# An adaLN modulation product in plain fp32 on four 32-column groups of the TensorE array, in place of two fp32r parts on the whole array

## The chip, the cores and the metric

The kernel runs on one core of a Trainium2 chip. The metric is the device time of one execution in microseconds; the lower the better. The engines are TensorE (PE; its weight loads are shown as PEld), VectorE (DVE), ScalarE (ACT), GpSimd (POOL) and SyncE (SP), whose queue issues the loads and stores.

## The reference, cut to what matters

One step of a decoder layer for 1024 prompt tokens and 64 sample tokens, model width 2048, all in float32. The modulation comes from a small batch of 9 vectors c (one for the prompt, eight for the samples):

```python
mod = jax.nn.silu(c) @ w_ada + b_ada              # (9, 2048) @ (2048, 6144)
shift, scale, gate = jnp.split(mod[:, None, :], 3, axis=-1)
xn = rmsnorm(x, norm_g) * (1.0 + scale) + shift
z = xn @ w_in                                     # (tokens, 2048) @ (2048, 5120)
...
out = jnp.concatenate([ya, yb, yc], axis=-1) @ w_out
return x + gate * out, new_hist_a, h_last, new_hist_b, vn
```

What lies between z and out are three token mixers (a linear recurrence, a causal convolution, a chunked spatial gate). w_ada is 50 MB, a quarter of all that the kernel loads.

## The kernel before, in words

Activations lie with channels on the 128 partitions and tokens along the free dimension. The tokens are done in two parts, first 512 prompt tokens (T0), then 512 prompt and 64 sample tokens (T1). Each large product is made of fp32r matmuls: an fp32 operand is split into a high part (a cast to fp32r on ScalarE, L98) and the rest (a subtraction on VectorE, L99), and three matmuls add up high x high, high x low and low x high (`mm3`, L132 to L134). The moving operand is the activations, 512 columns for T0.

The modulation product (w_ada) is done the other way round: the stationary operand is c after its SiLU, the moving one is w_ada. The weights are laid out in 24 pieces n of 256 output columns; each piece has 4 blocks b of 512 KB, and each block holds 4 tiles of 128 rows (k = 4b + j) side by side. n = 0 to 7 give shift, 8 to 15 scale, 16 to 23 gate.

- `cs` (L92, filled at L138 to L143) holds for each k 18 columns, the high part of 9 vectors and the low part of the same; `ada_mm` takes 128 columns from there as the stationary operand, of which the first 18 count.
- `ada_block` (L683) loads a block to a ring of 6 buffers ("ar"), splits it in two halves to high and low on ScalarE and VectorE, and calls `ada_mm`: 4 x 2 matmuls with 256 columns, which all add to one PSUM tile, high and low rows apart.
- `ada_fin` (L164) copies rows 0 to 18 of that tile to SBUF, and turns them by two small fp32 matmuls against `sel`, which adds high and low rows (`ps_adat`, L170); VectorE adds the bias and writes `adam`, the modulation by channel.
- `gate_block` (L156) does the same for n = 16 to 23, later: after each half of a `single` product of part T0 from the 19th on, one block, loaded and split by `load_w` (L101).

The first stage (the loop `for i in range(9)` near the end) goes through i = 0 to 8: the blocks of n = i and n = 8 + i, and, from i = 1 on, the normalised activations 2(i-1) and 2(i-1)+1 (`norm_pair`) and their first projection step (`k_step`: 18 matmuls with 512 columns to `ps_g`). The statistics of the norm need all 16 tiles of x (`load_x0`: squares on ScalarE, 14 additions on VectorE into two accumulators, then L711 adds these two), a reduction on TensorE (`ps_var`, L211) and a row broadcast (`ps_bc`, L202). 18 small VectorE steps of a softplus series (`sw`) are independent of all that.

The order on each engine is set by a scheduler that takes priorities (`tc.high_priority`) and the readiness of data as it estimates it; each engine then works strictly by its list.

Of the kernel before, what the change touches and what calls it, by code (L numbers as in the profile page):

```python
# [8 lines left out]
F32 = mybir.dt.float32  # L9
F32R = mybir.dt.float32r  # L10
AF = mybir.ActivationFunctionType
ALU = mybir.AluOpType
PSUM = bass.MemoryType.PSUM

P = 128
KT = 16
# [4 lines left out]
TM = T1  # L21
# [22 lines left out]
def decoder_layer(ctx: ExitStack, tc: tile.TileContext, a):  # L44
    nc = tc.nc

    cpool = ctx.enter_context(tc.tile_pool(name="cpool", bufs=1))
    xp = ctx.enter_context(tc.tile_pool(name="xp", bufs=17))
# [10 lines left out]
    HP = 4000  # L59
# [15 lines left out]
    ident = cpool.tile([P, P], F32, name="ident")  # L75
    make_identity(nc, ident)
    sel = cpool.tile([P, 9], F32, name="sel")
    nc.vector.tensor_tensor(sel[0:18, :], ident[0:18, 0:9], ident[0:18, 9:18], op=ALU.add)
    one_d = cpool.tile([P, 1], F32, name="one_d")
    nc.gpsimd.memset(one_d, 1.0 / 2048.0)  # L80
    one_c = cpool.tile([P, P], F32, name="one_c")
# [7 lines left out]
    car_h = cpool.tile([P, 8], F32, name="car_h")  # L89
    car_glu = cpool.tile([P, 4, 30], F32, name="car_glu")  # L90
    hs_out = cpool.tile([P, 8, 8], F32, name="hs_out")
    cs = cpool.tile([P, KT * 18 + 110], F32R, name="cs")  # L92
    nc.gpsimd.memset(car_xa, 0.0)
    nc.gpsimd.memset(car_h, 0.0)
    nc.gpsimd.memset(car_glu, 0.0)
# [1 line left out]
    def split(raw, hi, lo):  # L97
        nc.scalar.copy(hi, raw)  # L98
        nc.vector.tensor_tensor(lo, raw, hi.bitcast(F32), op=ALU.subtract)  # L99
# [35 lines left out]

    with tc.high_priority(10 * HP):
        sg = ap.tile([P, KT, 9], F32, tag="sg", name="sg", bufs=1)
        nc.scalar.activation(sg, cT, AF.Sigmoid)  # L138
        nc.vector.tensor_tensor(sg, sg, cT, op=ALU.mult)
        nc.gpsimd.memset(cs[:, KT * 18:].bitcast(F32), 0.0)  # L140
        cs3 = cs[:, :KT * 18].rearrange("p (k n) -> p k n", n=18)
        nc.scalar.copy(cs3[:, :, 0:9], sg)
        nc.vector.tensor_tensor(cs3[:, :, 9:18], sg, cs3[:, :, 0:9].bitcast(F32), op=ALU.subtract)  # L143

    def ada_mm(ps, b, hl):
        for j in range(4):
            k = 4 * b + j
            st = cs[:, k * 18:k * 18 + P]
            hi, lo = hl[j // 2]
            c = slice((j % 2) * 256, (j % 2) * 256 + 256)  # L150
            nc.tensor.matmul(ps, st, hi[:, c], start=(k == 0), stop=False)  # L151
            nc.tensor.matmul(ps, st, lo[:, c], start=False, stop=(k == 15))  # L152

    gate_ps = {}

    def gate_block(f):  # L156
        n, b = 16 + f // 4, f % 4
        if b == 0:
            gate_ps[n] = pmm.tile([P, 2, 512], F32, tag="mm", name="ps_ada")[:, 0, :256]
        ada_mm(gate_ps[n], b, load_w(a["w_ada"][n, b], 1024, 2))  # L160
        if b == 3:
            ada_fin(n, gate_ps[n])

    def ada_fin(n, ps):  # L164
        rows = stp.tile([P, 256], F32, tag="rows", name="rows", bufs=1)
        with tc.high_priority(HP):
            nc.scalar.copy(rows[0:18, :], ps[0:18, :])
        pt = mi("ps_adat")
        for j in range(2):
            nc.tensor.matmul(pt[:, j * 9:(j + 1) * 9], rows[0:18, j * P:(j + 1) * P],  # L170
                             sel[0:18, :], start=True, stop=True)
        with tc.high_priority(HP):
            dst = adam[:, n * 2:n * 2 + 2, :]
            o = VEC["b_ada"][0] + n * 2
# [506 lines left out]
    ada_ps = {}  # L681

    def ada_block(n, b):  # L683
        if b == 0:
            ada_ps[n] = mi("ps_ada")[:, :256]
        with tc.high_priority(HP):
            raw = ap.tile([P, 1024], F32, tag="ar", name="w_raw")
            nc.sync.dma_start(raw, a["w_ada"][n, b])
            hl = []
            for j in range(2):  # L690
                hi = xp.tile([P, TM], F32R, tag="xh", name="ada_hi")
                lo = xp.tile([P, TM], F32R, tag="xl", name="ada_lo")
                split(raw[:, j * 512:(j + 1) * 512], hi[:, :512], lo[:, :512])
                hl.append((hi, lo))
        ada_mm(ada_ps[n], b, hl)

    R0 = ap.tile([P, T0], F32, tag="R0", name="R0", bufs=1)
    o = VEC["h0"][0]
# [189 lines left out]
```

## Time and profile before

| what | value |
|---|---|
| median of 3 runs | 1559.56 us (1557.91 to 1559.74) |
| the profiled execution, span from its first to its last instruction | 1557.5 us |
| instructions | 24534 |
| TensorE busy | 1519.7 us, 9388 matmuls |
| TensorE weight loads | 1388.0 us |
| VectorE busy | 1038.4 us |
| ScalarE busy | 702.6 us |
| loaded and stored by DMA | 206.03 MB, mean 132 GB/s |

The profiled execution has no time of its own beside its span; the span lies 2.1 us under the median of the timed runs. Matmuls are pipelined and the end of each record is modelled: a matmul's length in a row is longer than its distance to the next. The distance between starts is what one costs. Each fp32 matmul of the code stands as two matmuls and two weight loads in the trace, an fp32r matmul as one.

### The profile page before, as it was taken

The numbers are of one execution on the slowest core, as the hardware profiler recorded it, in microseconds if no ns is written. First come the engines' busy times: TensorE is split into PE (matmuls) and PEld (weight loads), VectorE is DVE, ScalarE is ACT, GpSimd is POOL, SyncE is SP. The second block draws the span as 40 slices with busy tenths as digits, with TensorE's granted clock in tenths as the row PEclk, the third lists the DMA queues.
The fourth block names the chain that finished last, engine by engine and source line by source line (L and its number), as shares of the span: only waits on it lengthen the run. The fifth ranks groups of instructions, "written<-read, shape, count | busy, mean of one in ns | idle before, by whom it ended". The sixth has DMA issues, their size and how long they took to land.

```text
span 1557.5 us, 24534 instructions
## 1 busy us (share of the span) xinstructions
PE 1519.7 (98%) x9388; PEld 1388.0 (89%) x9388; DVE 1038.4 (67%) x1965; ACT 702.6 (45%) x1211; POOL 52.9 (3%) x120
## 2 busy tenths in 40 slices
PE   5999999999999999999999999999999999999996
PEld 4888788888887888888899999999999999999996
DVE  7888797397878756265595898358866753534345
ACT  6776442244666755244352432226254652422220
POOL 0000000001100100000000010001000000000000
PEclk7999999999999999999999999999999999999998
DMA  8888323323544453366466222222222222234323
GB/s 331 291 289 296 106 81 99 104 85 99 166 156 132 157 163 123 99 202 182 125 200 206 80 76 93 82 82 75 96 89 81 69 72 66 76 113 133 109 85 122
DMA packets 77334, 206.03 MB, mean 132 GB/s; under 512 B 9633, under 2 KB 25633, under 8 KB 77217
## 3 DMA queue, kind: packets, MB, share of 16 engines
q1 hardware_dynamic: 76064, 203.30, 39.5%
q8 instruction: 73, 1.20, 0.3%
q10 hardware_dynamic: 1152, 1.18, 0.2%
q14 instruction: 45, 0.36, 0.1%
HBM read 194.70 MB, written 9.74 MB: 131 GB/s over the span
## 4 chain that ended last, share of the span: by engine, by line
PE 64%; DVE 2%; ACT 1%; issue 0%; DVEq 0%; ACTq 0%
PE ps_s L132 16%; PE ps_s L134 16%; PE ps_s L133 16%; PE ps_g L132 5%; PE ps_g L133 5%; PE ps_g L134 4%; PE ps_bc L202 0%; DVE y L640 0%; PE ps_ada L151 0%; PE ps_ada L152 0%; PE ps_gate L132 0%; PE ps_var L211 0%; PE ps_gate L133 0%; PE ps_gate L134 0%; ACT L441 0%
## 5 line engine op out<-in xcount | busy, mean ns | idle before, releaser
L99 DVE TENSOR_TENSOR w_lo<-w_raw,w_hi 128x512 fp32r<-128x512 f32 (+1 forms) x544 | 351.6, 657 | 385.6 <-PE ps_s L134 239.3
L98 ACT CAST w_hi<-w_raw 128x512 fp32r<-128x512 f32 (+1 forms) x544 | 317.7, 594 | 633.4 <-PE ps_s L133 430.5
L132 PE MATMUL ps_s<-xn_hi,w_hi 128*128 128x288 f32 (+1 forms) x1632 | 535.8, 328 | 2.3 <-ACT pad_a L422 1.2
L133 PE MATMUL ps_s<-xn_lo,w_hi 128*128 128x288 f32 (+1 forms) x1632 | 534.3, 327 | 0.0
L134 PE MATMUL ps_s<-xn_hi,w_lo 128*128 128x288 f32 (+1 forms) x1632 | 533.4, 327 | 0.0
L132 PEld LDWEIGHTS ps_s<-xn_hi,w_hi 128*128 128x128 f32 x1632 | 306.2, 188 | 23.6 <-ACT pad_a L422 1.5
L134 PEld LDWEIGHTS ps_s<-xn_hi,w_lo 128*128 128x128 f32 x1632 | 307.1, 188 | 21.2
L133 PEld LDWEIGHTS ps_s<-xn_lo,w_hi 128*128 128x128 f32 x1632 | 306.5, 188 | 20.8 <-issue 0.5
L359 DVE SCALAR_TENSOR_TENSOR mx<-pad_b,vec,mx 128x512 f32<-128x512 f32 x240 | 177.5, 745 | 2.2
L132 PE MATMUL ps_s<-m_hi,w_hi 128*128 128x288 f32 (+1 forms) x480 | 157.2, 327 | 0.0
L133 PE MATMUL ps_s<-m_lo,w_hi 128*128 128x288 f32 (+1 forms) x480 | 156.7, 326 | 0.0
L134 PE MATMUL ps_s<-m_hi,w_lo 128*128 128x288 f32 (+1 forms) x480 | 156.5, 326 | 0.0
L132 PE MATMUL ps_g<-xn_hi,w_hi 128*128 128x288 f32 (+1 forms) x288 | 94.1, 332 | 2.5 <-ACT xn_hi L227 2.1
L134 PEld LDWEIGHTS ps_s<-m_hi,w_lo 128*128 128x128 f32 x480 | 90.3, 188 | 6.3
L133 PEld LDWEIGHTS ps_s<-m_lo,w_hi 128*128 128x128 f32 x480 | 90.1, 188 | 6.2
L132 PEld LDWEIGHTS ps_s<-m_hi,w_hi 128*128 128x128 f32 x480 | 90.1, 188 | 6.2
L133 PE MATMUL ps_g<-xn_lo,w_hi 128*128 128x288 f32 (+1 forms) x288 | 95.1, 331 | 0.0
L134 PE MATMUL ps_g<-xn_hi,w_lo 128*128 128x288 f32 (+1 forms) x288 | 94.4, 328 | 0.0
L132 PE MATMUL ps_g<-m_hi,w_hi 128*128 128x288 f32 (+1 forms) x288 | 94.1, 328 | 0.1
L133 PE MATMUL ps_g<-m_lo,w_hi 128*128 128x288 f32 (+1 forms) x288 | 94.0, 327 | 0.0
L134 PE MATMUL ps_g<-m_hi,w_lo 128*128 128x288 f32 (+1 forms) x288 | 93.7, 326 | 0.0
L99 DVE TENSOR_TENSOR ada_lo<-w_raw,ada_hi 128x512 fp32r<-128x512 f32 x128 | 80.4, 685 | 6.6 <-ACT ada_hi L98 6.5
(208 smaller groups left out, 1869.6 us busy)
## 6 DMA issues: line engine op xcount, KB each, us to landing
w_raw<-wi_s SPq DMA_DIRECT2D x136, 512.0 KB, 3.5
w_raw<-w_ada SPq DMA_DIRECT2D x96, 512.0 KB, 4.7
w_raw<-wo_s SPq DMA_DIRECT2D x40, 512.0 KB, 3.5
w_raw<-wi_g SPq DMA_DIRECT2D x16, 384.0 KB, 6.1
w_raw<-wo_g SPq DMA_DIRECT2D x16, 384.0 KB, 3.0
w_raw<-wi_g SPq DMA_DIRECT2D x32, 192.0 KB, 2.6
w_raw<-wo_g SPq DMA_DIRECT2D x32, 192.0 KB, 2.3
x_s<-x SPq DMA_DIRECT2D x16, 288.0 KB, 3.3
```

Source lines behind the costliest of these rows:

```text
L98: nc.scalar.copy(hi, raw)
L99: nc.vector.tensor_tensor(lo, raw, hi.bitcast(F32), op=ALU.subtract)
L132: nc.tensor.matmul(out, wh, xh, start=start, stop=False)
L133: nc.tensor.matmul(out, wh, xl, start=False, stop=False)
L134: nc.tensor.matmul(out, wl, xh, start=False, stop=stop)
L359: nc.vector.scalar_tensor_tensor(out[:, :T0], pad[:, j:j + T0], w[:, j:j + 1], out[:, :T0], op0=ALU.mult, op1=ALU.add)
```

## The change

The stationary operand is now a zero-padded fp32 tile `cz` with 32 columns for each k. `ada_mm` makes one plain fp32 matmul of 256 columns per k tile instead of two fp32r ones; the matmul of tile j writes PSUM partitions 32j to 32j + 31, that is, it uses the j-th group of 32 columns of the array. The four groups are added by the small product with `sel`, which now has 128 rows with four ones per column. The weights are no longer split: the casts, subtractions and the high and low tiles of w_ada are gone. In the gate stage a block is loaded in two pieces of 256 KB to a ring of four buffers ("xr") instead of one piece of 512 KB to the ring that the projection weights use.

```diff
-    nc.vector.tensor_tensor(sel[0:18, :], ident[0:18, 0:9], ident[0:18, 9:18], op=ALU.add)
+    nc.vector.tensor_tensor(sel, ident[:, 0:9], ident[:, 32:41], op=ALU.add)
+    nc.vector.tensor_tensor(sel, sel, ident[:, 64:73], op=ALU.add)
+    nc.vector.tensor_tensor(sel, sel, ident[:, 96:105], op=ALU.add)
...
-    cs = cpool.tile([P, KT * 18 + 110], F32R, name="cs")
+    cz = cpool.tile([P, KT, 32], F32, name="cz")
...
+        nc.gpsimd.memset(cz, 0.0)
         nc.scalar.activation(sg, cT, AF.Sigmoid)
         nc.vector.tensor_tensor(sg, sg, cT, op=ALU.mult)
-        nc.gpsimd.memset(cs[:, KT * 18:].bitcast(F32), 0.0)
-        cs3 = cs[:, :KT * 18].rearrange("p (k n) -> p k n", n=18)
-        nc.scalar.copy(cs3[:, :, 0:9], sg)
-        nc.vector.tensor_tensor(cs3[:, :, 9:18], sg, cs3[:, :, 0:9].bitcast(F32), op=ALU.subtract)
-
-    def ada_mm(ps, b, hl):
+        nc.vector.tensor_copy(cz[:, :, 0:9], sg)
+
+    def ada_mm(ps, b, raw):
         for j in range(4):
-            k = 4 * b + j
-            st = cs[:, k * 18:k * 18 + P]
-            hi, lo = hl[j // 2]
-            c = slice((j % 2) * 256, (j % 2) * 256 + 256)
-            nc.tensor.matmul(ps, st, hi[:, c], start=(k == 0), stop=False)
-            nc.tensor.matmul(ps, st, lo[:, c], start=False, stop=(k == 15))
+            nc.tensor.matmul(ps[32 * j:32 * j + 32, :], cz[:, 4 * b + j, :],
+                             raw[j // 2][:, j % 2 * 256:(j % 2 + 1) * 256],
+                             start=(b == 0), stop=(b == 3))
...
-        ada_mm(gate_ps[n], b, load_w(a["w_ada"][n, b], 1024, 2))
+        raw = []
+        with tc.high_priority(HP):
+            for q in range(2):
+                r = sp_.tile([P, TM], F32, tag="xr", name="g_raw")
+                nc.sync.dma_start(r[:, :512], a["w_ada"][n, b][:, q * 512:(q + 1) * 512])
+                raw.append(r)
+        ada_mm(gate_ps[n], b, raw)
...
-            nc.scalar.copy(rows[0:18, :], ps[0:18, :])
+            nc.scalar.copy(rows, ps)
...
-            nc.tensor.matmul(pt[:, j * 9:(j + 1) * 9], rows[0:18, j * P:(j + 1) * P],
-                             sel[0:18, :], start=True, stop=True)
+            nc.tensor.matmul(pt[:, j * 9:(j + 1) * 9], rows[:, j * P:(j + 1) * P],
+                             sel, start=True, stop=True)
...
             nc.sync.dma_start(raw, a["w_ada"][n, b])
-            hl = []
-            for j in range(2):
-                hi = xp.tile([P, TM], F32R, tag="xh", name="ada_hi")
-                lo = xp.tile([P, TM], F32R, tag="xl", name="ada_lo")
-                split(raw[:, j * 512:(j + 1) * 512], hi[:, :512], lo[:, :512])
-                hl.append((hi, lo))
-        ada_mm(ada_ps[n], b, hl)
+        ada_mm(ada_ps[n], b, [raw[:, :512], raw[:, 512:]])
```

The change also moves instructions, since the scheduler no longer sees the splits. On TensorE in the first stage, around the first two projection steps, the matmuls of one n stood between those of the projection before (L151 and L152 are the high and low part of the modulation product, L132 to L134 the projection):

```order
L132 MATMUL ps_g<-xn_hi,w_hi 128x512 x3
L133 MATMUL ps_g<-xn_lo,w_hi 128x512 x2
L134 MATMUL ps_g<-xn_hi,w_lo 128x512
L132 MATMUL ps_g<-xn_hi,w_hi 128x512
L151 MATMUL ps_ada<-ada_hi,cs 128x256
L133 MATMUL ps_g<-xn_lo,w_hi 128x512
L134 MATMUL ps_g<-xn_hi,w_lo 128x512 x2
```

Now the 16 matmuls of one n stand in one piece, here n = 8 + 1 behind the first projection step (L147 is the modulation product, L173 the small product that turns it, L134 to L136 the projection):

```order
L136 MATMUL ps_g<-xn_hi,w_lo 128x512
L147 MATMUL ps_ada<-w_raw,cz 32x256 x16
L173 MATMUL ps_adat<-sel,rows 128x9 x2
L134 MATMUL ps_g<-xn_hi,w_hi 128x512
L135 MATMUL ps_g<-xn_lo,w_hi 128x512
```

The count per n falls from 32 to 16, and full-width and 32-column matmuls alternate by n, no longer one by one.

On TensorE in the gate stage the four matmuls of a block stand between full-width matmuls of a `single` product, as the eight did before:

```order
L135 MATMUL ps_s<-xn_lo,w_hi 128x512
L136 MATMUL ps_s<-xn_hi,w_lo 128x512
L147 MATMUL ps_ada<-g_raw,cz 32x256 x4
L134 MATMUL ps_s<-xn_hi,w_hi 128x512
L135 MATMUL ps_s<-xn_lo,w_hi 128x512
```

There are 32 such blocks, each alone.

On VectorE at the start, the steps of the softplus series (`sw`) stood between the additions of the squares (`acc`) and the subtractions (L99):

```order
L667 TENSOR_TENSOR acc_115<-acc_115,x_sq 128x512
L99 TENSOR_TENSOR ada_lo<-w_raw,ada_hi 128x512
L667 TENSOR_TENSOR acc_114<-acc_114,x_sq 128x512
L667 TENSOR_TENSOR acc_115<-acc_115,x_sq 128x512
L667 TENSOR_TENSOR acc_114<-acc_114,x_sq 128x512
L748 TENSOR_SCALAR sw_2026<-sw_2026 128x8
```

Now all of the series that follows the first `adam` stands ahead of the first addition of the squares:

```order
L178 TENSOR_TENSOR adam<-ps_adat,vec 128x18
L744 TENSOR_TENSOR sw_1259<-sw_1259,sw_1258 128x8
...
L746 TENSOR_TENSOR sw_1259<-sw_1259,sw_1257 128x8
L748 SCALAR_TENSOR_TENSOR sp_100<-sw_1259,sw_1256 128x8
L749 TENSOR_SCALAR sp_100<-sp_100 128x8
L750 TENSOR_SCALAR nsp_101<-sp_100 128x8
L670 TENSOR_TENSOR acc_115<-acc_115,x_sq 128x512
L670 TENSOR_TENSOR acc_116<-acc_116,x_sq 128x512
```

The additions moved behind 18 small steps, and the subtractions between them are gone.

## Rows read from the trace of the kernel before

**Rows 1.** The page, busy time of each engine (share of the span).

```profile
PE 1519.7 (98%) x9388; PEld 1388.0 (89%) x9388; DVE 1038.4 (67%) x1965; ACT 702.6 (45%) x1211; POOL 52.9 (3%) x120
```

**Rows 2.** Stages: length, busy time by engine, granted clock, DMA share, GB/s.

```profile
core 0: us, PE busy (x) PEld busy (x) DVE busy (x) ACT busy (x) POOL busy (x), PEclk, DMA share, GB/s
0.00:40.00 40.00, 22.08 (x112) 20.18 (x113) 29.10 (x78) 28.24 (x52) 1.24 (x12) 0.74 0.89 332
40.00:155.00 115.00, 114.97 (x715) 99.81 (x714) 99.68 (x181) 81.54 (x162) 0.17 (x1) 1.00 0.81 291
386.00:606.00 220.00, 218.71 (x1090) 182.96 (x1089) 164.82 (x269) 144.21 (x238) 15.24 (x25) 1.00 0.46 150
```

**Rows 3.** Timeline of TensorE (start, length), first stage: one n and what follows.

```profile
63.07 0.39 PE L151 MATMUL ps_ada<-ada_hi,cs 128*128 128x256 f32 x1
...
66.95 0.39 PE L132 MATMUL ps_g<-xn_hi,w_hi 128*128 128x512 f32 x1
```

**Rows 4.** Timeline of TensorE, gate stage: one block and what follows.

```profile
387.12 0.28 PE L151 MATMUL ps_ada<-w_hi,cs 128*128 128x256 f32 x1
...
388.07 0.39 PE L132 MATMUL ps_s<-xn_hi,w_hi 128*128 128x512 f32 x1
```

**Rows 5.** Groups by line, 0 to 160 us: busy, mean ns | idle before.

```profile
L99 DVE TENSOR_TENSOR ada_lo<-w_raw,ada_hi 128x512 fp32r<-128x512 f32 x128 | 80.4, 685 | 6.6 <-ACT ada_hi L98 6.5
L98 ACT CAST ada_hi<-w_raw 128x512 fp32r<-128x512 f32 x128 | 70.4, 615 | 9.9 <-PE ps_ada L151 6.8 <-DMA w_raw<-w_ada 3.0
```

**Rows 6.** Timeline of TensorE around the mean of a layernorm, an fp32 matmul.

```profile
176.07 1.10 PE L293 MATMUL ps_mean<-ln_s,one_c 128*128 128x512 f32 x2
176.60 0.79 PE L132 MATMUL ps_s<-xn_hi,w_hi 128*128 128x512 f32 x1
177.24 0.39 PE L133 MATMUL ps_s<-xn_lo,w_hi 128*128 128x512 f32 x1
```

**Rows 7.** Timeline of the weight loads at the same place.

```profile
176.58 0.19 PEld L132 LDWEIGHTS ps_s<-xn_hi,w_hi 128*128 128x128 f32 x1 [0.24 <-issue]
177.01 0.19 PEld L133 LDWEIGHTS ps_s<-xn_lo,w_hi 128*128 128x128 f32 x1 [0.24 <-issue]
177.24 0.19 PEld L134 LDWEIGHTS ps_s<-xn_hi,w_lo 128*128 128x128 f32 x1
```

**Rows 8.** Timeline of TensorE, gate stage: the 18-row matmuls between full ones.

```profile
409.39 0.39 PE L132 MATMUL ps_s<-xn_hi,w_hi 128*128 128x512 f32 x1
409.71 0.61 PE L170 MATMUL ps_adat<-sel,rows 18*128 18x9 f32 x4
410.25 0.50 PE L133 MATMUL ps_s<-xn_lo,w_hi 128*128 128x512 f32 x1
410.58 0.40 PE L134 MATMUL ps_s<-xn_hi,w_lo 128*128 128x512 f32 x1
```

**Rows 9.** Groups by form, weight loads of 96 and of 128 columns.

```profile
L211 PEld LDWEIGHTS ps_var<-one_c,ln_s 128*96 128x96 f32 x24 | 2.2, 165 | 0.0
...
L211 PEld LDWEIGHTS ps_var<-one_c,ln_s 128*128 128x128 f32 x16 | 1.9, 191 | 0.6 <-issue 0.3 <-PE ps_s L133 0.3
```

**Rows 10.** Timeline of TensorE, start: the reduction of the squares (idle before it).

```profile
17.63 0.41 PE L152 MATMUL ps_ada<-ada_lo,cs 128*128 128x256 f32 x1
26.55 1.84 PE L211 MATMUL ps_var<-one_d,acc 128*128 128x1 f32 x8 [8.51 <-DVE acc L711]
28.25 0.56 PE L151 MATMUL ps_ada<-ada_hi,cs 128*128 128x256 f32 x1
```

**Rows 11.** Timeline of VectorE, start: modulation, series and squares.

```profile
14.72 0.18 DVE L175 TENSOR_TENSOR adam<-ps_adat,vec 128x18 f32<-128x18 f32 x1 [0.40 <-PE ps_adat L170]
...
19.38 0.16 DVE L747 TENSOR_TENSOR sw<-sw,sw 128x8 f32<-128x8 f32 x1
19.57 0.17 DVE L748 TENSOR_SCALAR sw<-sw 128x8 f32<-128x8 f32 x1
...
25.71 0.69 DVE L711 TENSOR_TENSOR acc<-acc,acc 128x512 f32<-128x512 f32 x1
```

**Rows 12.** The modulation's PSUM tile: duration min/median/max, first and last start.

```profile
L152 PE MATMUL ps_ada<-ada_lo,cs x256: 274/281/582, 7.1 to 155.1; 128*128 128x256 f32 x128
```

## Prediction

> **What bounds the kernel now.** I read the page's busy times first, then the table of stages, then the engine's own sequence in the two stages that the change touches. TensorE is busy for 98% of the span [rows 1]. [...]
>
> The two prices of today: one n (256 output columns: 4 blocks, 32 matmuls of 256 columns, high and low part of each k tile) takes from 63.07 to 66.95 us, **3.88 us** [rows 3]. One gate block (8 matmuls) takes from 387.12 to 388.07, **0.95 us** [rows 4]. At full clock that is 0.12 us a matmul. These matmuls are of type fp32r.
>
> **The change, part by part.**
>
> *Removed on ScalarE and VectorE.* 128 casts of 615 ns and 128 subtractions of 685 ns in the first stage [rows 5], and 64 of each in the gate stage. TensorE hides them from 40 us on, so I cost them at nothing there. If that cover were gone the DMA would be late next: rows 2 give 40 x 332 + 115 x 291 = 46.7 MB up to 155 us, and 332 GB/s at a share of 0.89 makes some 373 GB/s at most, so the loads alone need about 125 us (estimate).
>
> *One fp32 matmul instead of two fp32r ones.* A plain fp32 matmul of full width stands in the trace in the mean of the layernorms. It is recorded as two matmuls with a weight load each. The second starts at 176.58 (the load for the work behind it is issued at that moment), and the load after that one is issued at 177.01, when the second pass is through and the matmul behind it begins to stream [rows 6, 7]: 0.43 us for 512 columns, so about **0.214 us for 256**, twice per matmul. One k tile thus costs 0.43 us of its columns of the array, against 0.24 now. The change pays only if column groups run side by side.
>
> *How many run side by side.* No row shows a group of 32 columns. The bounds are none (16 matmuls x 0.43 = 6.85 us for one n) and all four (4 blocks x 0.43 = 1.71 us). I take **two**, for this reason: the two passes of one matmul use the same columns, and TensorE takes its matmuls in order. Rows 10 show the order: the reduction that waits 8.51 us for VectorE holds up the modulation matmuls behind it. The order of issue after the change is pass 1 and pass 2 of group 0, then of group 1, and so on. Pass 2 of group 0 must wait for its pass 1; only then can pass 1 of group 1 enter, beside it; its pass 2 waits again. Each matmul advances the queue by one pass. Between two groups there is also a weight load: the loads of 96 and 128 columns take 165 and 191 ns, some 25 ns per 32 columns [rows 9], and in the trace a load starts when the matmul before it starts (177.24 on both) [rows 6, 7], so I add 0.025: 0.239 us per matmul. Bounds for that load: 0, and 0.135, the step of the small 9-column fp32 passes with full loads (0.54 us for four) [rows 8].
>
> *Changing the array's shape.* The one neighbour is the 18-row matmul between full ones [rows 8]: it starts at 409.71, 0.09 after the matmul of 409.39 would have made room (0.23 each), and the one after it takes 0.33 instead of 0.23. So **0.19 us** for each excursion; 0 is the other bound. [...]
>
> *First stage from 45 us on.* Three of the 16 n (0, 8, 1) belong to the start; 13 remain. One n: 16 x 0.239 + 0.214 + 0.19 = 4.23 us instead of 3.88, 0.35 more: 13 x 0.35 = **+4.5 us**. The order shows the 16 matmuls of one n in one piece, so each n pays one excursion.
>
> *Gate stage.* Here each block stands alone between full matmuls: 4 x 0.239 + 0.214 + 0.19 = 1.36 us instead of 0.95: 32 x 0.41 = **+13.1 us**. The two loads of 256 KB per block wait in SyncE's queue for the block two before; the weight loads behind them there are four halves ahead of their use, so TensorE is not held.
>
> *Start.* The first matmul no longer waits for a cast and two more steps (a memset of POOL and a copy come instead): it may start 1 to 2 us sooner, but then waits for the blocks. What sets the start is VectorE's chain of squares: it ends with the addition of 25.71, and the reduction follows at 26.55 [rows 10, 11]. Without the subtractions the chain could end sooner, but the order shows that the 18 small steps of the softplus series now stand in a row ahead of the 14 additions: from about 13.4 (the first n done, 14.72 now) 18 x 0.19 + 14 x 0.69 [rows 11] end at about 26.5. Nothing is won there; the half-clock matmuls that follow are 11 and 16 with the estimated 0.48 and 0.24 us each. I take **-1 us** (bounds -8 and +8: all four groups side by side, or none).
>
> *Small things.* Two more VectorE additions for sel (0.15 us each, off the path), the copy of 128 rows instead of 18 (same length, 256 columns), and the transposing product with 128 rows (9 columns as before): nothing.
>
> **Sum:** -1 + 4.5 + 13.1 = +16.6. The span of the profiled execution is 1557.5; the median of the runs, 1559.56, lies 2.06 higher, which I add: 1557.5 + 16.6 + 2.1 = **1576 us**. The range of this case alone: with no load between groups, no cost of shape and -3 for the start it is 13 x -0.24 + 32 x 0.12 - 3 = -2.3, so 1557; with 0.135 for the load 13 x 2.1 + 32 x 0.85 + 2 = +56.5, so 1616.
>
> **Rivals.**
>
> *All four groups side by side (faster).* If a pass that waits for its own columns does not hold up the next group, one n takes 1.71 + 0.025 + 0.19 = 1.93 (13 x -1.95 = -25.4) and a gate block 0.43 + 0.025 + 0.19 = 0.64 (32 x -0.31 = -9.9); the start gains 8 because the blocks are no longer waited for. The last modulation matmul, now at 155.1 [rows 12], would come at about 122, which is the DMA's 125, so 3 are lost again: -40, **1519 us**. For it: the groups share no columns and no PSUM partitions, and the order puts the four next to each other. Against it: the two recorded passes per matmul and the order that rows 10 show. It decides from 0.18 us per matmul down. [...]
>
> *Nothing side by side (slower still; the change doesn't do what it says).* One n: 6.85 + 0.19 = 7.04 (13 x 3.16 = +41); a gate block 1.71 + 0.19 = 1.90 (32 x 0.95 = +30.4); the start is delayed by about 8, since the first n then ends near 20 us and VectorE's steps wait for it: +79, **1639 us**. For it: no row shows two matmuls that stream at once. Against it: a load that runs beside a matmul in every full-width row. [...]
>
> **How the numbers follow.** Two at a time 0.55, all four 0.25, none 0.20. A measurement of this kernel can tell about 0.2% (3.1 us) from no change. Of the first case 0.04 lies below 1556.4 and 0.08 within 3.1 us of 1559.6; so faster 0.29, same 0.08, slower 0.63. The likeliest case alone has the range 1557 to 1616. Leaving out the last rival, the range is 1516 to 1614.
>
> **What the profile will show.** The step from one modulation matmul pair to the next in the stage after 45 us: near 0.24 us per matmul (two at a time), 0.11 (four) or 0.43 (none); one n near 4.2 us, a gate block near 1.36; the reduction of the squares still near 26 us; ScalarE and VectorE some 80 us less busy each before 160 us, with no gain from that. I am wrong if the granted clock falls during the small groups (I count full clock from 40 us on, as now [rows 2]), if the shape change costs several times 0.19, or if TensorE waits for loads in the gate stage.

## The result, and the profile after

The changed kernel takes **1529.21 us** (median of 4 runs, 1527.73 to 1530.43), against 1558.74 (1556.78 to 1559.74) for the kernel before on the same chip: ratio 0.9815, 95% interval 0.9801 to 0.9829, some 29 us faster. The forecast was 1576 us, slower; the rival with all four groups side by side said 1519. The whole range of 1516 to 1614 us held the time because it held that rival too; the likeliest case alone said 1557 to 1616, and the time is not in it.

The busy times of the page after (before: [rows 1]):

```profile
PE 1480.3 (97%) x9388; PEld 1308.0 (86%) x9388; DVE 927.0 (61%) x1775; ACT 602.9 (39%) x1018; POOL 49.7 (3%) x120
```

TensorE is busy for 39.4 us less, the span falls by 28.8 (1557.5 to 1528.7). So some 10 us of what TensorE saved came back as idle time, and the next view says where: the stages of the kernel after (start, busy times, granted clock, DMA share, GB/s; before: [rows 2]).

```profile
0.00:40.00 40.00, 20.96 (x133) 10.99 (x134) 19.65 (x62) 18.21 (x30) 1.57 (x12) 1.00 0.92 337
40.00:138.00 98.00, 88.03 (x695) 58.18 (x693) 31.37 (x66) 23.86 (x51) 0.60 (x4) 1.00 0.88 321
367.00:576.00 209.00, 208.48 (x1085) 154.39 (x1083) 129.59 (x207) 111.92 (x176) 9.98 (x25) 1.00 0.46 157
```

In the first stage, where TensorE had been busy throughout, it is now idle for 9.97 of 98 us. In the gate stage it stays busy. The clock of 1.00 in the first row is not what ran: the trace's first clock event lies at 36.76 us, and what lies ahead of it counts as full. Passes of 256 columns stand 0.427 us apart there up to 36.1 us and 0.216 us from 42.5 on, so the start still ran at half pace (the trace of the kernel before shows a granted clock of 0.50 from 15 to 30 us). In the same way the 0.74 of [rows 2] counts the 11.4 us ahead of the first event as full.

How the gain divides is read from the first ps_s of the kernel, the border between the first stage and the rest (one tile: duration min/median/max, first and last start in the first 400 us). In the kernel before:

```profile
L132 PE MATMUL ps_s<-xn_hi,w_hi x311: 387/389/792, 171.1 to 399.9; 128*128 128x512 f32 x156
```

And after:

```profile
L134 PE MATMUL ps_s<-xn_hi,w_hi x336: 387/389/792, 151.2 to 399.6; 128*128 128x512 f32 x168
```

Up to there the kernel gains 19.9 us; behind it 1557.5 - 171.1 = 1386.4 becomes 1528.7 - 151.2 = 1377.5, **8.9 us**.

The 19.9 us are not all the modulation product's. Three rows of the kernel before (its first ps_g, the second n behind that of [rows 3], and what follows the last n), and one of the kernel after (its first ps_g):

```profile
40.02 0.86 PE L132 MATMUL ps_g<-xn_hi,w_hi 128*128 128x512 f32 x3
...
80.41 0.39 PE L151 MATMUL ps_ada<-ada_hi,cs 128*128 128x256 f32 x1
...
161.18 1.34 PE L132 MATMUL ps_g<-xn_hi,w_hi 128*128 128x512 f32 x3 [2.08 <-ACT xn_hi L227]
```

```profile
37.77 0.48 PE L134 MATMUL ps_g<-xn_hi,w_hi 128*128 128x512 f32 x1
```

The first ps_g comes 2.2 us earlier. Two n with their k-steps (a k-step is the 18 matmuls of one projection step) took 80.41 - 63.07 = 17.34 us and now take 104.15 - 88.69 = 15.46 (the rows below), 0.94 less per n and **12.2 us** for 13 n. Behind the last n the kernel before waited 2.08 us for xn_hi and then ran for a while at half pace (granted clock 0.50 from 162 to 165 us), which cost it 1.5 us more (36 ps_g took 9.90 us up to the first ps_s, against 8.40 in the kernel with two groups below); the kernel after has neither. These make 18.0 of the 19.9; 1.9 are not assigned.

TensorE's timeline after, first stage, one n and the k-step that follows (start, length, engine, line, count, idle before), to be set beside [rows 3]:

```profile
88.69 1.93 PE L147 MATMUL ps_ada<-w_raw,cz 128*32 128x256 f32 x32
91.17 0.61 PE L173 MATMUL ps_adat<-sel,rows 128*128 128x9 f32 x4 [0.55 <-ACT rows L170]
91.64 0.48 PE L134 MATMUL ps_g<-xn_hi,w_hi 128*128 128x512 f32 x1
...
93.52 0.50 PE L136 MATMUL ps_g<-xn_hi,w_lo 128*128 128x512 f32 x1 [0.48 <-DVE w_lo L101]
...
96.69 1.93 PE L147 MATMUL ps_ada<-w_raw,cz 128*32 128x256 f32 x32
...
104.15 1.93 PE L147 MATMUL ps_ada<-w_raw,cz 128*32 128x256 f32 x32
```

The 16 matmuls of one n (32 recorded passes) span 1.93 us by their record, whose end is modelled. The figure to set beside the 3.88 of before is the distance to the next matmul where nothing is waited for, 1.86 us (44.34 to 46.20 in the last kernel of the experiments). Then two new waits stand in the row: for the copy of the 128 rows (0.55 us ahead of ps_adat, in each n), and, in the k-step of every second n, for the low part of the projection's weights (0.48).

One gate block after, and a transposing product, to be set beside [rows 4, 8]:

```profile
387.16 0.39 PE L136 MATMUL ps_s<-xn_hi,w_lo 128*128 128x512 f32 x1
387.48 0.64 PE L147 MATMUL ps_ada<-g_raw,cz 128*32 128x256 f32 x8
388.05 0.50 PE L134 MATMUL ps_s<-xn_hi,w_hi 128*128 128x512 f32 x1
388.39 0.39 PE L135 MATMUL ps_s<-xn_lo,w_hi 128*128 128x512 f32 x1
388.62 0.39 PE L136 MATMUL ps_s<-xn_hi,w_lo 128*128 128x512 f32 x1
388.85 0.40 PE L134 MATMUL ps_s<-xn_hi,w_hi 128*128 128x512 f32 x1
389.08 0.51 PE L173 MATMUL ps_adat<-sel,rows 128*128 128x9 f32 x4
389.45 0.48 PE L135 MATMUL ps_s<-xn_lo,w_hi 128*128 128x512 f32 x1
389.76 0.40 PE L136 MATMUL ps_s<-xn_hi,w_lo 128*128 128x512 f32 x1
```

From its start to the next ps_s a block takes 0.57 us, against 0.95. A ps_s between its like takes 0.23; the one ahead of the block takes 0.32 and the one behind it 0.34. So the block costs 388.62 - 387.16 - 3 x 0.23 = 0.77 us in all, some 0.18 less than before.

The single records of that block (start in us, length in ns; two passes for each of the four groups) show why:

```
387.480  403   first passes, groups 0 to 3
387.486  403
387.493  403
387.500  403
387.720  379   second passes, groups 0 to 3
387.726  379   (posts a semaphore)
387.733  379
387.740  379   (posts a semaphore)
```

The four first passes start within 20 ns, the four second passes 0.24 us later. Which is which is told by the semaphores: the first and the third record wait for the two halves of the block, so the first four are the tiles 0 to 3, and the second and the fourth matmul post theirs with their second passes. If the two passes of a matmul are issued one after the other, as the prediction took it, the second pass of a group stands ahead of the first pass of the next one. **The passes of different groups run side by side, and out of that order**; the second experiment shows it for whole matmuls, whatever the order of the passes.

### The profile page after: what moved, and what is told of

Same layout as the page of the kernel before. It is cut to its first block, busy times and chain, and to the rows that moved or that the text cites. A ratio compares the mean times of both kernels' runs of the same rounds, so it can differ in the third digit from the quotient of the medians.

```text
span 1528.7 us, 23924 instructions
## 1 busy us (share of the span) xinstructions
PE 1480.3 (97%) x9388; PEld 1308.0 (86%) x9388; DVE 927.0 (61%) x1775; ACT 602.9 (39%) x1018; POOL 49.7 (3%) x120
## 4 chain that ended last, share of the span: by engine, by line
PE 93%; DVE 3%; DMA 1%; issue 1%; ACT 1%; SPq 0%; POOL 0%; DVEq 0%; ACTq 0%
PE ps_s L134 23%; PE ps_s L135 22%; PE ps_s L136 22%; PE ps_g L136 6%; PE ps_g L134 6%; PE ps_g L135 6%; PE ps_ada L147 3%; PE ps_adat L173 1%; PE ps_bc L205 1%; PE ps_gate L134 1%; DVE w_lo L101 1%; PE ps_var L214 1%; PE ps_gate L135 0%; DVE y L643 0%; DMA w_raw<-w_ada 0%
## 5 line engine op out<-in xcount | busy, mean ns | idle before, releaser
L101 DVE TENSOR_TENSOR w_lo<-w_raw,w_hi 128x512 fp32r<-128x512 f32 (+1 forms) x480 | 311.9, 653 | 407.6 <-PE ps_s L136 265.5
L134 PE MATMUL ps_s<-xn_hi,w_hi 128*128 128x288 f32 (+1 forms) x1632 | 538.4, 330 | 1.9 <-ACT pad_a L425 1.2
L100 ACT CAST w_hi<-w_raw 128x512 fp32r<-128x512 f32 (+1 forms) x480 | 281.8, 591 | 649.5 <-PE ps_s L135 452.2
L136 PE MATMUL ps_s<-xn_hi,w_lo 128*128 128x288 f32 (+1 forms) x1632 | 532.7, 326 | 0.0
L134 PEld LDWEIGHTS ps_s<-xn_hi,w_hi 128*128 128x128 f32 x1632 | 306.0, 188 | 33.3 <-issue 7.5
L136 PEld LDWEIGHTS ps_s<-xn_hi,w_lo 128*128 128x128 f32 x1632 | 307.1, 188 | 21.4
L134 PE MATMUL ps_s<-m_hi,w_hi 128*128 128x288 f32 (+1 forms) x480 | 157.1, 327 | 0.0
L136 PE MATMUL ps_s<-m_hi,w_lo 128*128 128x288 f32 (+1 forms) x480 | 156.4, 326 | 0.0
L136 PE MATMUL ps_g<-xn_hi,w_lo 128*128 128x288 f32 (+1 forms) x288 | 94.3, 332 | 3.3 <-DVE w_lo L101 3.3
L134 PE MATMUL ps_g<-xn_hi,w_hi 128*128 128x288 f32 (+1 forms) x288 | 96.0, 333 | 1.2 <-ACT mx L482 0.9
L136 PEld LDWEIGHTS ps_s<-m_hi,w_lo 128*128 128x128 f32 x480 | 90.3, 188 | 6.3
L134 PEld LDWEIGHTS ps_s<-m_hi,w_hi 128*128 128x128 f32 x480 | 90.0, 188 | 6.2
L134 PE MATMUL ps_g<-m_hi,w_hi 128*128 128x288 f32 (+1 forms) x288 | 94.2, 328 | 0.1
L136 PE MATMUL ps_g<-m_hi,w_lo 128*128 128x288 f32 (+1 forms) x288 | 93.6, 326 | 0.0
L136 PEld LDWEIGHTS ps_g<-xn_hi,w_lo 128*128 128x128 f32 x288 | 54.1, 188 | 12.4 <-DVE w_lo L101 9.0
```

The lines of the kernel that those rows point to most:

```text
L134: nc.tensor.matmul(out, wh, xh, start=start, stop=False)
L136: nc.tensor.matmul(out, wl, xh, start=False, stop=stop)
```

## The experiments

The theory from here on: four groups run side by side, the price of the product is TensorE's alone, and what the rival's 1519 us lacks are the two waits in the first stage. Times are medians where there were several runs; the kernel before took 1556.9 to 1557.9 beside them.

**Two groups in place of four** (1555.98 us, one run). The second half of each block goes to the groups of the first half again; the copy and the product with `sel` take the 64 rows that are left.

```diff
-            nc.tensor.matmul(ps[32 * j:32 * j + 32, :], cz[:, 4 * b + j, :],
+            nc.tensor.matmul(ps[32 * (j % 2):32 * (j % 2) + 32, :], cz[:, 4 * b + j, :],
...
-                             start=(b == 0), stop=(b == 3))
+                             start=(b == 0 and j < 2), stop=(b == 3 and j > 1))
...
```

> Only two column groups are used, in the order 0, 1, 0, 1 within a block (the tile j goes to group j mod 2). Theory A (each column group works through its own matmuls; groups do not wait for each other) and theory B (TensorE takes matmuls strictly in order, and the four were side by side only because first passes came before second ones) expect the same here: a gate block takes 4 passes of 0.214 us, 0.86 us instead of 0.43 (with its ends 0.57 became about 1.0 us), 32 x 0.43 = +14 us; one n in the first stage takes 16 passes, 3.4 us instead of 1.7, 13 x 1.7 = +22 us. Together 1529 + 36 = 1565 us. If the loads and not TensorE set the first stage's period, most of the +22 would be absorbed: about 1545 us.

One n of this kernel on TensorE, and what follows:

```profile
66.79 3.65 PE L147 MATMUL ps_ada<-w_raw,cz 128*32 128x256 f32 x32
70.37 0.50 PE L134 MATMUL ps_g<-xn_hi,w_hi 128*128 128x512 f32 x1
...
83.66 3.65 PE L147 MATMUL ps_ada<-w_raw,cz 128*32 128x256 f32 x32
```

And its first ps_s (as above):

```profile
L134 PE MATMUL ps_s<-xn_hi,w_hi x320: 387/389/792, 161.5 to 398.3; 128*128 128x512 f32 x160
```

3.58 us for 32 passes: 16 pairs of 0.216, and 0.12 more. The records of a pair start 7 ns apart. A gate block takes 0.99 us. Casts and subtractions of w_ada are gone here as in the changed kernel, TensorE's price per n is about that of before (3.88), and the time is about that of before. But the equal time is a sum of two parts that offset each other. The first ps_s comes 9.6 us earlier than before, of which 2.9 lie ahead of the first ps_g (37.08) and 3.1 in 13 n (two n take 16.87 us against 17.34); behind it the kernel takes 1554.3 - 161.5 = 1392.8 us, 6.4 more, since a gate block now costs 0.99 and some 0.20 in its neighbours against 0.95. So per n, from 40 us on, taking work from ScalarE and VectorE gave nothing that shows beyond the little by which TensorE's own matmuls are shorter; what it gave at the start is not separated. The expectation of 1565 was missed by 9 us: the order of this kernel sets ps_adat behind the k-step, so the two waits of the first stage are gone, and the first ps_s comes 10.3 us later than in the changed kernel instead of 22.

**The same two groups, in the order 0, 0, 1, 1** (1559.65 us, one run).

```diff
-            nc.tensor.matmul(ps[32 * (j % 2):32 * (j % 2) + 32, :], cz[:, 4 * b + j, :],
+            nc.tensor.matmul(ps[32 * (j // 2):32 * (j // 2) + 32, :], cz[:, 4 * b + j, :],
...
-                             start=(b == 0), stop=(b == 3))
+                             start=(b == 0 and j % 2 == 0), stop=(b == 3 and j % 2 == 1))
...
```

> The same two column groups in the order 0, 0, 1, 1 within a block. Theory A: the order does not matter, the same time as with 0, 1, 0, 1 within 2 us, and a gate block of about 1.0 us. Theory B: a pass that waits for its own group holds up the other group, 5 to 7 passes per block instead of 4: a gate block of 1.2 to 1.6 us, some 7 to 20 us more in the gate stage and 9 to 28 us more in the first stage, 16 to 48 us above the run with 0, 1, 0, 1.

One n takes 3.60 us, a gate block 0.99, and the passes of the two groups still start 13 to 30 ns apart, although four passes of group 0 now stand ahead of the first one of group 1. In a gate block the second record (387.417, 14 ns behind the first) is the one that waits for the block's second half, so it is tile 2; tile 1, issued ahead of it, starts 0.24 us later or more. Strict order would have made the gate block 1.2 us or longer, by the expectation's count of passes. The total is 3.7 us above that of the order 0, 1, 0, 1, more than the 2 us expected; 2.2 of it lie ahead of the first ps_g (39.26 against 37.08), and each kernel ran once, so it can't be put down to the order. This kernel contradicts the step of the prediction on its own terms: the waiting passes of tile 1 did not hold up the first pass of tile 2, which is for other columns.

**One group for each block** (1608.8 us, one run): block b of an n goes to group b, so eight passes of one group stand ahead of the next group's.

```diff
-            nc.tensor.matmul(ps[32 * j:32 * j + 32, :], cz[:, 4 * b + j, :],
+            nc.tensor.matmul(ps[32 * b:32 * b + 32, :], cz[:, 4 * b + j, :],
...
-                             start=(b == 0), stop=(b == 3))
+                             start=(j == 0), stop=(j == 3))
```

> Four column groups, but the group is the block's number b and not the tile's j: the four matmuls of a block all use one group, and groups change only from block to block. In the gate stage a block stands alone, so both theories expect it serial: 8 passes, 1.71 us instead of 0.43, 32 x 1.28 = +41 us. In the first stage the 16 matmuls of one n stand together as 0000 1111 2222 3333. Theory A with a far look-ahead (8 passes of one group do not hold up the next): one n still takes about 1.7 us, total 1570 us. Theory B, or A with a short look-ahead: the n takes near 32 passes, 6.8 us, 13 x 5.1 = +66 us more, total 1637 us.

Neither number came out, but one between them: one n takes 5.1 us from its first pass to ps_adat (62.66 to 67.77, of which 0.52 are the wait for the rows copy). The single records say when the next group gets in:

```
62.661  403   block 0, pass 1
62.901  379   block 0, pass 2
63.117  379   block 0, pass 3
63.333  379   block 0, pass 4
63.549  379   block 0, pass 5
63.555  403   block 1, pass 1
63.765  379   block 0, pass 6
63.795  379   block 1, pass 2
```

Block 1 enters with the fifth pass of block 0, 0.89 us late, and block 2 with the fifth of block 1 (64.448). It is no wait for data: the loads of the three blocks behind block 0 had landed by 60.1 us. So in both cases the next group's first pass started with the fifth of the eight passes ahead of it, 0.89 us after the first of them; in the change itself no such run of passes stands in the way.

**The change in the gate stage alone** (1548.93 us; 0.9943 of before, 0.9929 to 0.9956). The first stage splits w_ada as before.

```diff
...
-        ada_mm(gate_ps[n], b, load_w(a["w_ada"][n, b], 1024, 2))
...
+            nc.tensor.matmul(ps[32 * j:32 * j + 32, :], cz[:, 4 * b + j, :],
+                             raw[j // 2][:, j % 2 * 256:(j % 2 + 1) * 256],
+                             start=(b == 0), stop=(b == 3))
...
```

> Edit: the kernel before with the change made in the gate stage alone (32 blocks there in plain fp32 on four groups; the first stage splits w_ada as before). Theory A (the two stages gain independently, 20 us in the first and 9 us behind it, by the start of the first ps_s and the span of the two traces): 1548 to 1551 us against 1557 to 1559. Rival I (part of the 9 us came from loads and low parts that the shorter first stage set in another order, so that the gate blocks alone give 32 x 0.19 us at most): 1552 to 1557 us.

8.9 us less than before, as the split of the two traces said: the gate stage gains this without the change in the first stage. 32 blocks x 0.18 = 5.8 of it are the blocks; the eight transposing products there cost 0.45 each with 128 rows (0.37, and 0.08 in the ps_s behind) against some 0.73 with 18 rows [rows 8], 2.2 more. The remaining 0.9 is not assigned.

**Casts and subtractions put back, unused** (1534.56 us; 0.9852 of before, 0.9837 to 0.9867).

```diff
+            for j in range(2):
+                hi = xp.tile([P, TM], F32R, tag="xh", name="ada_hi")
+                lo = xp.tile([P, TM], F32R, tag="xl", name="ada_lo")
+                split(raw[:, j * 512:(j + 1) * 512], hi[:, :512], lo[:, :512])
         ada_mm(ada_ps[n], b, [raw[:, :512], raw[:, 512:]])
```

> Edit: the first stage again casts and subtracts every 128x1024 block of w_ada on ScalarE and VectorE, as the kernel before did, but the product still takes the raw block; the parts are thrown away. The build also moves ps_adat of every second n behind the k-step's 18 matmuls. Theory P (the gain is TensorE's alone, casts and subtractions lay beside it before and would again): 1523 to 1532 us. Rival V (the gain of the first stage came from the engines relieved: VectorE would have about 15 us of work in a period of 15.5 us for two n, so norms and low weights come later still): 1535 to 1545 us.

Between the two: this kernel is some 6 us slower than the changed one (0.9852 against 0.9815), of a gain of 29. That is a net figure, since the order of ps_adat changed as well and removes the wait for the rows copy in about half of the n, so the casts and subtractions alone may cost more. TensorE's waits from 42 to 138 us have another cast in them (engine, line, what it waited for: us in total, times, longest):

```profile
PEld ps_adat L173 <- ACT rows L170: 7.1, 7, 1.0
PEld ps_g L136 <- DVE w_lo L101: 6.4, 7, 1.4
PEld ps_g L134 <- ACT w_hi L100: 5.3, 5, 2.2
```

The first of these in the changed kernel:

```profile
PEld ps_adat L173 <- ACT rows L170: 13.4, 13, 1.0
```

The wait for the high part of the weights is new: ScalarE's casts of w_ada stand ahead of it. The profiled execution loses only 1.8 us of the 6 (1530.5 against 1528.7); the rest is in the spread of the runs and not located.

**Weights loaded and split ahead of the four blocks** (1550.77 us; 0.9963, 0.9949 to 0.9977).

```diff
...
+            if i > 0 and f % 4 == 0:
+                k_load(2 * (i - 1) + f // 4)
             if i < 8:
                 ada_block(n, f % 4)
```

(k_load loads and splits the weights of one k-step.)

> The load and split of a projection step's weights is written ahead of the four modulation blocks that precede the step, nothing else is changed; the scheduler then also sets the modulation matmuls between those of the projection. Theory W (the first stage's period of 15.5 us is set by TensorE's waits: 0.9 us per n for the copy of the modulation's rows and 0.3 to 0.9 us for low weights that ScalarE casts only behind that copy): the waits go, more excursions to column groups come (0.2 us each), the period falls to 13.4 to 14 us, total 1529 - 10 to 14 = 1515 to 1519 us. Rival D (the loads set the period): no change, 1527 to 1531 us.

Some 21 us slower than the change as it stands; both expectations missed. With the weights early the k-step's matmuls are ready while blocks are still being loaded, and the build sets the blocks one by one between them. TensorE's timeline in the first stage:

```profile
81.86 0.40 PE L136 MATMUL ps_g<-xn_hi,w_lo 128*128 128x512 f32 x1
82.19 0.64 PE L147 MATMUL ps_ada<-w_raw,cz 128*32 128x256 f32 x8
82.76 0.50 PE L134 MATMUL ps_g<-xn_hi,w_hi 128*128 128x512 f32 x1
...
85.38 0.64 PE L147 MATMUL ps_ada<-w_raw,cz 128*32 128x256 f32 x8
87.47 1.04 PE L134 MATMUL ps_g<-xn_hi,w_hi 128*128 128x512 f32 x3 [1.45 <-ACT xn_hi L230]
88.31 0.80 PE L135 MATMUL ps_g<-xn_lo,w_hi 128*128 128x512 f32 x1
```

A block alone pays 0.77 us, as in the gate stage, four of them 3.1; a run of 16 takes 1.86 us to the next matmul where nothing is waited for (44.34 to 46.20 in the last kernel below), about 2.1 in all with its neighbours. And the chain from ps_adat over adam and x to xn_hi, which the waits had covered, is now waited for in every second n (1.45 us), in some of them with matmuls at half pace behind it, as here (the granted clock is 0.91 from 80 to 100 us in this kernel).

**Half of the w_ada traffic** in the first stage (1519.38 us; 0.9753, 0.9739 to 0.9768), and **a ring of 7 blocks** in place of 6 (1527.28 us; 0.9806, 0.9791 to 0.9820).

```diff
-            nc.sync.dma_start(raw, a["w_ada"][n, b])
+            nc.sync.dma_start(raw[:, :512], a["w_ada"][n, b][:, :512])
...
```

> Edit: in the first stage only the first 512 of 1024 columns of each block of w_ada are loaded and both halves of the product read them, so half of the first stage's w_ada is left out of the result and of the traffic. The build also sets ps_adat of every second n behind the 18 matmuls of its k-step. Theory W (TensorE's waits for the rows copy, some 0.9 us in each n, and for low weights, up to 0.5 us, are what is left; the loads wait in the ring but are not waited for): the reordering alone saves 0.9 us in half of 13 n and some of the waits for low weights, 1519 to 1526 us. Rival D (the loads set the period of 15.5 us for two n, at a DMA share of 0.87): with half the w_ada traffic the period falls to TensorE's own 12.5 to 13.3 us, 6.5 x 2.2 to 3 us less: 1509 to 1515 us.

```diff
-    apool = tc.tile_pool(name="apool", bufs=6)
+    apool = tc.tile_pool(name="apool", bufs=7)
```

> Edit: the ring that takes the w_ada blocks has 7 buffers in place of 6, so SP issues one load further ahead; TensorE's order in the first stage stays 16 matmuls, ps_adat, 18 matmuls. Theory W (loads are not waited for): 1527 to 1531 us, no change. Rival D (TensorE is held up by loads that wait for a free buffer, 64 us of SP's waiting in the first stage): 1519 to 1525 us.

The ring changes nothing that these runs can tell from the 0.9815 of the change, and two n still take 15.44 us in its trace (78.56 to 94.00). Half the loads give 10 us, at the lower end of theory W's range and 4 us above rival D's; but this build also sets every second ps_adat behind the 18 matmuls of its k-step, so alone it doesn't say which. The next kernel does, with all the loads.

**The rows copy later** (**1518.96 us**; 0.9751, 0.9734 to 0.9767).

```diff
...
+            if i > 0 and f % 4 == 3:
+                k_load(2 * (i - 1) + f // 4)
             if i < 8:
                 ada_block(n, f % 4)
...
-                    k_step(2 * (i - 1) + f // 4)
-                if i < 8:
+                    k_step(2 * (i - 1) + f // 4, i < 8 and (lambda: ada_fin(n, ada_ps[n])))
+                elif i < 8:
```

(k_step calls its second argument ahead of its third column.)

> Edit: the k-step's weights are loaded and split ahead of the fourth block of w_ada, and the rows copy and ps_adat are set after two of the k-step's six columns; TensorE's order becomes 12 matmuls of ps_ada, 5 of ps_g, 4 of ps_ada, 3 of ps_g, ps_adat, 10 of ps_g. Theory W: it saves 0.9 us of wait for the rows copy and 0.1 to 0.5 us for low weights in each of 13 n and pays two more changes of shape of some 0.3 us each: 13 x 0.4 to 0.8 us less, 1518 to 1525 us. Rival N (the chain from ps_adat over adam, x and xn_hi to the next k-step takes the wait's place, as it did with early weights, 1.45 us in every second n): 1527 to 1536 us.

The stage between 40 and 130 us (columns as above):

```profile
40.00:130.00 90.00, 90.00 (x699) 57.78 (x698) 33.26 (x71) 25.16 (x54) 0.60 (x4) 1.00 0.94 345
```

One n of it on TensorE:

```profile
90.02 1.50 PE L147 MATMUL ps_ada<-w_raw,cz 128*32 128x256 f32 x24
91.45 0.50 PE L134 MATMUL ps_g<-xn_hi,w_hi 128*128 128x512 f32 x1
...
92.81 0.64 PE L147 MATMUL ps_ada<-w_raw,cz 128*32 128x256 f32 x8
...
94.19 0.51 PE L173 MATMUL ps_adat<-sel,rows 128*128 128x9 f32 x4
...
97.01 1.50 PE L147 MATMUL ps_ada<-w_raw,cz 128*32 128x256 f32 x24
```

TensorE waits for nothing in this stretch, one n with its k-step takes 6.99 us in place of 7.73 (half of 104.15 - 88.69), and the same loads go through at a higher share. So the loads did not bind; the rows copy and the weights did. That the time is the rival's 1519 is in part luck: this kernel pays two more changes of shape in each n than the one that the rival priced.

**The same, ring of 7, gate blocks in 16 pairs** (**1514.99 us**; 0.9725, 0.9712 to 0.9739: the fastest here).

```diff
...
-                    (lambda h: gate_block(g0 + h)) if g0 >= 0 else None)
+                    (lambda h: h and (gate_block(g0), gate_block(g0 + 1))) if g0 >= 0 else None)
```

> Edit: the kernel with the late rows copy, its ring of w_ada blocks at 7 buffers, and the 32 gate blocks set in 16 pairs (8 matmuls in one run in place of 4 and 4). Theory S (a block set alone pays 0.57 us and some 0.19 us in the ps_s after it, a block inside a run of four 0.39 us: the change of tile shape costs about 0.37 us): 16 changes fewer, 16 x 0.37 = 5.9 us less, and 0 to 1.5 us for the ring: 1511 to 1514 us against 1519. Rival L (a pair takes all four buffers of the xr ring at once, so its loads come late and TensorE waits for them): 1518 to 1526 us.

A pair on TensorE's timeline:

```profile
387.74 0.39 PE L136 MATMUL ps_s<-xn_hi,w_lo 128*128 128x512 f32 x1
388.05 1.07 PE L147 MATMUL ps_ada<-g_raw,cz 128*32 128x256 f32 x16
389.05 0.50 PE L134 MATMUL ps_gate<-xac_h,s_hi 128*128 128x512 f32 x1
```

The time lies just above what theory S expected. Two blocks take 1.00 us to the next matmul where two single ones take 2 x 0.57; with what the neighbours pay (0.09 and 0.11, as around a single block) that is 1.20 against 2 x 0.77, 0.34 less for a pair. The spans of the two profiled executions differ by 5.5 us (1518.0 and 1512.5), of which 0.6 lies ahead of the first ps_s (140.7 and 140.1); 4.9 over 16 pairs make **0.31 us** for a change of shape, there and back. The medians of the runs are only 4.0 us apart, which would make it 0.21, so 0.3 is good to about 0.1.

**All 16 matmuls of an n in one run** (1541.21 us; 0.9897, 0.9881 to 0.9914). On top of the last kernel, the block that is loaded last is multiplied first.

```diff
...
+            for q in (3, 0, 1, 2):
+                ada_mm(ada_ps[n], q, [ada_raw[q][:, :512], ada_raw[q][:, 512:]], 3, 2)
...
```

> Edit: the kernel with gates in pairs; in the first stage the block that is loaded last is now multiplied first, so that the 16 matmuls of an n stand in one run again (16 of ps_ada, 3 of ps_g, ps_adat, 15 of ps_g) in place of 12, 5, 4, 3, ps_adat, 10. Theory S (a change of shape costs 0.37 us): one change fewer in 13 n, 4.8 us less, some 0.2 us of it lost per n because the rows copy now has only three ps_g to hide behind: 1509 to 1513 us against 1515. Rival D (the loads bind below a period of 14 us for two n: at a DMA share of 0.94 they moved 345 GB/s, so at most some 367, and 4.98 MB for two n take 13.6 us): 1512 to 1517 us, with ps_ada waiting for w_raw.

Some 26 us slower than the kernel that it stands on, and a miss of both expectations by 24 us or more. It is not the price of the run: where nothing is waited for, 16 matmuls take 1.86 us to the next ps_g.

```profile
44.34 1.93 PE L147 MATMUL ps_ada<-w_raw,cz 128*32 128x256 f32 x32
46.20 0.50 PE L134 MATMUL ps_g<-xn_hi,w_hi 128*128 128x512 f32 x1
```

The loss lies in the first stage, for the first ps_s comes at 165.1 instead of 140.1. It is not rival D either: from 40 us to there no matmul of ps_ada waits for a load. The new order puts ps_adat right ahead of matmuls that need its result in every second n. TensorE's timeline there:

```profile
98.26 0.61 PE L173 MATMUL ps_adat<-sel,rows 128*128 128x9 f32 x4 [0.55 <-ACT rows L170]
100.89 1.65 PE L134 MATMUL ps_g<-xn_hi,w_hi 128*128 128x512 f32 x3 [2.02 <-ACT xn_hi L230]
102.33 0.63 PE L135 MATMUL ps_g<-xn_lo,w_hi 128*128 128x512 f32 x1
102.76 0.63 PE L136 MATMUL ps_g<-xn_hi,w_lo 128*128 128x512 f32 x1
...
103.97 0.39 PE L136 MATMUL ps_g<-xn_hi,w_lo 128*128 128x512 f32 x1
104.19 0.39 PE L135 MATMUL ps_g<-xn_lo,w_hi 128*128 128x512 f32 x1
```

Two stretches of the same kernel, ahead of the wait and around it:

```profile
90.00:95.00 5.00, 5.00 (x24) 4.20 (x25) 1.21 (x3) 1.30 (x3) 0.00 (x0) 1.00 0.89 308
98.00:105.00 7.00, 4.72 (x16) 3.84 (x17) 4.22 (x8) 2.52 (x5) 0.00 (x0) 0.76 0.90 344
```

The wait of 2 us is paid for once more in part: behind it the matmuls start 0.43 us apart instead of 0.23, and the granted clock of the stretch is 0.76, where it was 1.00 ahead of it. The 13 ps_g up to the next run of ps_ada (105.45) take 4.56 us, some 1.5 more than at 0.23 each. Not every such wait has this behind it: in the kernel with two groups TensorE waits 2.02 us for xn_hi up to 153.12, and the 36 ps_g that follow take 8.40 us, 0.23 each.

## Why the prediction was wrong, step by step

- **How many run side by side: the step that failed.** "I take **two**, for this reason: the two passes of one matmul use the same columns, and TensorE takes its matmuls in order." The first half holds: the passes of one group are 0.216 us apart. The second doesn't, across groups: the records of a block (first passes of four groups within 20 ns, second passes 0.24 us later), and the kernel with the order 0, 0, 1, 1, show later passes for other columns overtaking. (So "each engine then works strictly by its list", in the section on the kernel before, does not hold for TensorE's matmuls of different column groups.) The row behind the step [rows 10] was a matmul of full width that waited for a semaphore; it says nothing of a matmul that waits for columns. With four side by side, one n is 16 x 0.43 / 4 = 1.71 us of passes and not 3.8, and a gate block 0.43. Of the sum, the first stage's +4.5 became -12.2 for the 13 n, and the gate stage's +13.1 became -8.9.
- **The pass** of 0.214 us (from the fp32 mean [rows 6, 7]): measured 0.216.
- **The load between groups**, 0.025 us per matmul: it doesn't appear. Starts of neighbouring groups lie 7 ns apart, also where only two groups are used in turn.
- **The change of shape**, taken at 0.19 us: about 0.3 by the gates in pairs (0.31 by the spans, 0.34 by the rows, 0.21 by the medians). Probably too low, though its nearest row was a fair one.
- **First stage.** The rival's price for one n, 1.93 us, was near (1.86 to the next matmul where nothing is waited for, about 2.06 with the neighbours). Its -30 for the stage and start became -19.9. Per n it had -1.95; the product gives 3.88 - 2.06 = 1.82, but the wait for the rows copy takes back 0.62 (2.48 to ps_adat instead of 1.86) and the low weights half of 0.48, since it had no term for a copy behind a shorter run, nor for low weights that come later than a faster TensorE wants them. 0.96 is left, and 0.94 is what the rows show. The kernel with the later rows copy gets back 10 us of this (first ps_s at 140.7 instead of 151.2). The loads, which the rival charged with 3 us, were not what bound. The 3.6 us that the kernel before loses behind its last n, by a wait and at half pace, stood in no case of the prediction.
- **Gate stage.** The rival's 32 x -0.31 = -9.9 stands against -8.9. That it comes so near is luck: the block saves less (0.18), and the transposing product with 128 rows, costed at nothing, saves 0.28 each time.
- **Casts and subtractions, costed at nothing:** right from 40 us on for a TensorE as slow as before, as the two-group kernels show (casts gone, and an n is shorter by no more than its own matmuls). In the faster one they are worth some 6 us net by the runs, as the put-back shows, and 1.8 by the profiled executions.
- **Start.** The reduction of the squares starts at 25.64, against 26.55 [rows 10], as the row of the softplus steps ahead of the additions said. The first ps_g comes 2.2 us earlier, so the prediction's -1 was near, and the rival's -8 was not. TensorE's timeline after:

```profile
25.64 1.83 PE L214 MATMUL ps_var<-one_d,acc 128*128 128x1 f32 x8 [1.18 <-DVE acc L708]
```

- **Clock and loads in the gate stage:** no loss, as forecast: granted clock 1.00, TensorE busy for 208.48 of 209 us.
- **The chances.** 0.25 for all four side by side was too little: no row of the trace spoke against it, only a row on another kind of wait.

## What to carry to other kernels

A product with few output rows can go on column groups, with the raw fp32 data if the split is only there for the speed of single matmuls: here four groups bring the two passes of fp32 below the price of two full-width passes (1.86 us for one n against 3.88), and two groups only just (3.58). Set neighbouring matmuls on different groups, and in long runs, since each change of shape cost about 0.3 us here; then look at what a shorter run uncovers, here the copy of its result and the weights of the next step. A wait of TensorE cost more than its own length where the granted clock fell behind it (2.02 us and some 1.5 more in the last kernel, at a clock of 0.76), so an order with no wait can beat one with fewer changes (1514.99 us against 1541.21 in the last two kernels).

## What the runs showed of the hardware

- Passes for different column groups overtook each other: 32 passes in 1.86 us (58 ns each) against 0.216 us for a pass by itself. With eight passes of one group in a row, the next group entered with the fifth (63.555 us, 0.89 after the first).
- A transposing product of 128 rows cost less between full matmuls than the same with 18 rows: 0.37 us to the next matmul against 0.54 [rows 8].
- Matmuls behind a wait of 2 us ran at about half pace for 2.7 us (100.89 to 103.61), with a granted clock of 0.76 in the 7 us around them. Behind a wait of the same length in the kernel with two groups they kept full pace (36 matmuls in 8.40 us).
